# Longer dense runs in a planned instruction order: twelve matmuls to a piece, fewer pages held back, no preference for dense work, and one column moved to ScalarE

## The chip, the cores and the metric

The kernel runs on one core of a Trainium2 chip. The metric is the time of one execution in microseconds (us), as the device reports it; lower is better. TensorE appears as PE, its weight loads as PEld, VectorE as DVE, ScalarE as ACT, GpSimd as POOL and the engine that issues the DMAs as SP.

## The reference

One layer of a streaming encoder on 1024 prompt rows and 32 sample rows of width 1024, float32 throughout. Cut to what matters:

```python
n = rmsnorm(x, lw['norm_mix'])
p = n @ lw['w_in']                                   # 1024 -> 3840 columns
hg_o, hg_s = hgrn2_mixer(p[..., :HG_COLS], ...)      # 4 heads of 128, gated linear recurrence
rw_o, rw_s, rw_shift = rwkv7_mixer(p[..., HG_COLS:], shift0, ...)   # 8 heads of 64
x = x + jnp.concatenate([hg_o, rw_o], axis=-1) @ lw['w_out']
x = x + cross_attend(rmsnorm(x, lw['norm_cross']), mk, mv, lw['w_cq'], lw['w_co'])
n = rmsnorm(x, lw['norm_ffn'])
x = x + (jax.nn.silu(n @ lw['w_ff1']) * (n @ lw['w_ff3'])) @ lw['w_ff2']
```

The first step of the RWKV mixer blends each projected row with the row before it, and this is where the one column comes from:

```python
prev = jnp.concatenate([shift0.astype(p.dtype), p[:, :-1]], axis=1)
xs = (p + (prev - p) * mu).astype(jnp.float32)
```

Both recurrences are computed in chunks, the RWKV one with an inversion of a 64x64 triangular matrix in every chunk and a chain of states from chunk to chunk.

## The kernel before, in words

The 1056 rows lie along the free axis, in three blocks of 352 (`BLOCKS`), four of 264, or chunks of 256, as a stage needs. A weight matrix times activations is a **dense product**: both operands are split into a high and a low float32r part, and `gemm` (or `fast` in the feed-forward) issues three matmuls per 128 rows of contraction: high by high, high by low, low by high. All other matmuls are small: transposes, 64x64 products of the state chain, float16 products of the inversion, scores and values of the attention.

The code does not fix the order of instructions. Every call is recorded as a node of a graph (`Graph.record`). Tensor calls up to the next `nc.cut()` form one node and stay together, so `if i % CUT == 0: nc.cut()` in `gemm` and `k % CUT` in `fast` set the length of a dense piece: with `CUT = 2`, two steps of contraction, six matmuls. `plan` then lists the nodes of all engines greedily in the order of modelled time, and `order` calls it up to `PASSES` times, each time with the latest start times (`latest`) of the result before as ranks, and keeps the pass with the shortest modelled span. The number that it minimises is a model's and is not used here.

What in `plan` bears on the change:

- Phases 0 (projections and mixers) to 6 are open at once within limits (`LEAD`), so dense work of one stage fills gaps in the chains of another.
- When a tensor node is picked, candidates that are ready go by rank. If more than `WARM = 2.0` us of modelled time have passed since the last dense node (`lack`), dense candidates go first.
- On-chip memory is a set of regions cut in pages. A node other than the oldest unfinished one gets pages only if `RESERVE[phase]` pages stay free (a third of it where the node also takes a PSUM bank): 64 in phase 0, 32 in phase 1.
- A tensor node takes one of 8 PSUM banks, kept until its readers are done.

`rw_proj` is the mixing step. For each of 14 column tiles and each block, `mix` reads the projected block from its PSUM bank: ACT writes the block times (1 - mu), DVE adds mu times the block shifted by one column. The first column of a block needs the last of the block before, which ACT keeps as `edge`; DVE adds it in an instruction of one column. In the last block the first sample row takes the shift row of the input (`sh`), again one column on DVE. `params` prepares per-column constants, `mixers` four scaled matrices `rkj`.

In traces and in the instruction order the names are those of the regions: `bank` is a PSUM bank; `f_0`, `mb` hold float32 tiles; `r_0` activations in float32r; `rw` weights in float32r. A PE instruction that reads `rw` is a dense one. All engine calls are issued from one line of `emit` (L378).

Of the kernel before, what the change touches and what calls it, by code (L numbers as in the profile page):

```python
# [30 lines left out]
BIAS = 1e5  # L31
TQ = T // 4
DIAG = 1
CUT = 2
WARM = 2.0
LATER = 10.0
PASSES = 3
KEEP = 1.5 * BIAS
FF_GROUPS = (3, 3, 2, 2)

# [19 lines left out]

REGIONS = {"f0": (192, "left", "FFFFFFF", ()), "wr": (32, "left", "FFFFFFF", ()), "r0": (192, "left", "RRRRRRR", ()), "rw": (64, "left", "RRRRRRR", ()),
           "mb": (256, "left", "FRRRRRR", (150,)), "r1": (64, "right", "RRRRFFF", (150,))}
RESERVE = [64, 32, 24, 24, 24, 24, 24]
AHEAD = {"rw": 1, "rc": 2, "hg": 2, "at": 3}
LEAD = {0: BIG, 1: 400, 2: 250, 3: 400, 4: 100, 5: 200, 6: 60}
HOME = {"keep": ("f0",), "wr": ("wr",), "wh": ("rw",), "wl": ("rw",), "wr2": ("wr",), "wh2": ("rw",), "wl2": ("rw",),
# [231 lines left out]
class Graph:  # L298
# [90 lines left out]
    def order(self):  # L389

        nodes = self.nodes
        for n in nodes:
            if n.calls[0][0] == "memset" and not n.preds:
                later = [u for b in n.bufs for u in b.users if u.i > n.i and u.calls[0][0] != "memset"]
                if later:
                    n.preds.update({p: None for p in min(later, key=lambda u: u.i).preds if p.calls[0][0] != "memset"})
        base = {n: n.cost for n in self.nodes}
        bufs = list(dict.fromkeys(b for n in self.nodes for b in n.bufs))
        best, rank = None, None
        self.log = []  # L400
        for _ in range(PASSES):
            for n in self.nodes:
                n.cost = base[n]
                if n.unit:
                    n.unit[2] = 0
            for b in bufs:
                b.at = None
            try:
                out = self.plan(rank)
            except AssertionError:  # L410
                self.log.append(None)
                break
            self.log.append(self.span)
            if best is None or self.span < best[0]:
                best = self.span, out, [b.at for b in bufs], [(n.start, n.cost) for n in self.nodes]
            rank = self.latest(out)
        self.span = best[0]
        for b, at in zip(bufs, best[2]):
            b.at = at
        for n, t in zip(self.nodes, best[3]):  # L420
            n.start, n.cost = t
        return best[1]

    def latest(self, out):

# [22 lines left out]
    def plan(self, rank):  # L448
# [30 lines left out]
            n.path = n.path - n.bias if rank is None else -rank[n]  # L479
        engines = ("tensor", "vector", "scalar", "gpsimd", "sync")  # L480
        clock = dict.fromkeys(engines, 0.0)
        warm = 0.0
        port = 0.0
        ready = {e: [] for e in engines}
        when = {}
# [76 lines left out]
        def fits(n, start):  # L562

            first = n.i == oldest
            if not first and sum(rest[:n.phase]) > LEAD[n.phase]:
                return None
            if n.unit and not first and n.unit[1] >= base[n.unit[0]] + AHEAD[n.unit[0]]:
                return None
            new = [b for b in n.bufs if b.at is None and b.fixed is None]
            if not new:  # L570
                return start
            for c in FIFO:
                k = sorted(b.turn for b in new if b.cls == c)
                if k and (k != list(range(turn[c], turn[c] + len(k))) or live[c] + len(k) > FIFO[c]):
                    return None
            ps = sum(b.space == "PS" for b in new)
            if ps:
                free = sorted(t for t in banks if t < BIG)
                if len(free) < ps + (0 if first else 2):
                    return None  # L580
                start = max(start, free[ps - 1])
            sb = [b for b in new if b.space == "SB"]
            if sb:
                keep = 0 if first or sb[0].kind == "R" or sb[0].cls in HOME else RESERVE[n.phase] // 3 if any(b.space == "PS" for b in n.bufs) else RESERVE[n.phase]
                if np.count_nonzero((freed < BIG) & pages(sb[0])) < sum(b.units for b in sb) + keep:
                    return None
                for b in sb:
                    if b.at is None:
                        at = place(b, start)
                        if at is None:  # L590
                            return None
                        start = max(start, at[1])
            return start
# [26 lines left out]
        while len(done) < len(nodes):  # L620
            turn_over()
            best = None
            for e in engines:
# [4 lines left out]
                    continue  # L628

                pick = None  # L630
                lack = e == "tensor" and now - warm > WARM
                for t, n in sorted(ready[e], key=lambda r: (max(r[0], now), lack and not r[1].dense, -r[1].path)):
                    t = max(t, now, port) if n.port else max(t, now)
                    if pick is not None and t >= pick[0]:
                        break
                    s = fits(n, t)
                    if s is None:
                        continue
                    if pick is None or s < pick[0]:
                        pick = s, n  # L640
                    if s <= now:
                        break
# [16 lines left out]
            ready[e] = [r for r in ready[e] if r[1] is not n]  # L659
            n.start = start  # L660
            clock[e] = start + n.cost
            if e == "tensor" and n.dense:
                warm = clock[e]
            if n.port:
                port = clock[e] - (0.15 if e == "gpsimd" else 0.0)
            when[n] = start + n.cost + n.late
# [38 lines left out]
class Net:  # L705
# [91 lines left out]
    def params(self):  # L797
# [25 lines left out]
            return self.dp[:, at:at + k]  # L823

        V.tensor_scalar(derived("omu", 0, 14), self.P("mu", 0, 14), -1.0, 1.0, ALU.mult, ALU.add)
        V.tensor_scalar(derived("nkk", 14, 4), self.P("kk", 0, 4), -1.0, None, ALU.mult)
        V.tensor_scalar(derived("nw0", 42, 4), self.P("w0", 0, 4), -1.0, None, ALU.mult)
        V.tensor_scalar(derived("na0", 46, 4), self.P("a0", 0, 4), -1.0, None, ALU.mult)
# [646 lines left out]
    def mixers(self):  # L1475
# [11 lines left out]
        self.rkj = []  # L1487
        for j in range(4):
            self.rkj.append(self.mc.tile([128, 128], F32, name="rkj"))
            nc.vector.tensor_scalar(self.rkj[j], self.j64, self.P("rk", j), None, ALU.mult)  # L1490
        for j in (0, 2):
            self.rwkv(j)
            self.enter(None)
# [48 lines left out]
    def rw_proj(self, tile, done=None, bias=BIAS):  # L1542
# [5 lines left out]
        def mix(t0, n, ps):  # L1548
            nonlocal edge
            m = self.tmp([128, TB], "mixed")[:, :n]  # L1550
            S.activation(m, ps, AF.Copy, scale=self.P("omu", tile))
            c = min(TP - t0, n)
            if t0:
                V.scalar_tensor_tensor(m[:, 0:1], edge, mu, m[:, 0:1], ALU.mult, ALU.add)
            V.scalar_tensor_tensor(m[:, 1:c], ps[:, 0:c - 1], mu, m[:, 1:c], ALU.mult, ALU.add)
            if c == n:
                edge = self.tmp([128, 1], "edge")
                S.copy(edge, ps[:, n - 1:n])
            else:
                S.copy(self.last[:, tile:tile + 1], ps[:, c - 1:c])  # L1560
                S.copy(self.last[:, 14 + tile:15 + tile], ps[:, n - 1:n])
                V.scalar_tensor_tensor(m[:, c:c + 1], self.P("sh", tile), mu, m[:, c:c + 1], ALU.mult, ALU.add)
                V.scalar_tensor_tensor(m[:, c + 1:n], ps[:, c:n - 1], mu, m[:, c + 1:n], ALU.mult, ALU.add)
            if done:
                done(t0, n, m)
            else:
                nc.sync.dma_start(self.p_dram[:, 16 + tile, t0:t0 + n], m)
# [485 lines left out]
```

## Time and profile before

| what | value |
|---|---|
| median of 3 runs | 1875.8 us (1875.39 to 1876.47) |
| the profiled execution | 1872.31 us, of it the span of the trace 1870.6 us |
| mean granted clock of TensorE | 0.988 |
| busy share of PE, DVE, ACT, POOL | 96%, 69%, 44%, 32% |
| matmul records | 15439, of them 9984 dense |
| DMA | 201.88 MB, mean 108 GB/s |

The span runs from the first to the last instruction of the program; about 1.7 us of the execution lie around it. A float32 matmul that is not float32r leaves two records in the trace, so there are more records than matmuls. A timeline row gives the start, the length, the engine, what is written and read, the array's share (rows*columns), the shape and how many; a wait stands behind it in brackets. Matmul records overlap, so the time that a group takes is read from its start to the next group's start.

### The profile page before, as it was taken

Reading aid. Unit: us, or ns where it says so; the run is one execution under the profiler, and the core shown is the slowest. Engines: PE = TensorE matmul, PEld = TensorE weight load, DVE = VectorE, ACT = ScalarE, POOL = GpSimd, SP = SyncE. Lnnn points to the kernel's source line nnn. Section 1 sums busy time; section 2 is a strip of 40 time slices with the busy share of each in tenths; the row PEclk is TensorE's granted clock in tenths of the full one; section 3 lists DMA queues with packets and bytes.
Section 4 is the critical chain, followed back from the end, with each engine's and each line's share of the span. In section 5 each row is a group of like instructions: output and inputs, shape, how many; then the busy total and the mean of one; then the engine's idle time right before and its main releaser. Section 6 shows DMA issues by size and latency. Waiting matters only on the chain. (4 is left out here: it accounts for less than half of the span.)

```text
span 1870.6 us, 39378 instructions
## 1 busy us (share of the span) xinstructions
PE 1798.7 (96%) x15439; PEld 1689.5 (90%) x15439; DVE 1287.8 (69%) x2547; ACT 827.0 (44%) x1938; POOL 594.7 (32%) x764
## 2 busy tenths in 40 slices
PE   6899999999999999999999999999999999999898
PEld 5898888888788888999999999899999999999897
DVE  5347746887766678623654547798877777978997
ACT  5535527465454567633322346333333333653432
POOL 6234234354323433245000024523223223233321
PEclk9999999999999999999999999999999999999999
DMA  6364123222312136844111143133222224644622
GB/s 190 103 193 113 37 79 100 81 69 64 101 49 66 61 101 193 248 139 137 47 46 46 48 149 103 46 113 123 87 94 90 87 102 169 202 146 141 194 69 94
DMA packets 206314, 201.88 MB, mean 108 GB/s; under 512 B 18712, under 2 KB 191376, under 8 KB 206128
## 3 DMA queue, kind: packets, MB, share of 16 engines
q1 hardware_dynamic: 206128, 199.37, 34.3%
q8 instruction: 121, 1.98, 0.5%
q14 instruction: 65, 0.53, 0.1%
HBM read 139.66 MB, written 59.67 MB: 107 GB/s over the span
## 5 line engine op out<-in xcount | busy, mean ns | idle before, releaser
L378 PE MATMUL bank<-r,rw 128*128 128x264 f32 (+1 forms) x5952 | 927.6, 308 | 8.9 <-DVE mb L378 4.1
L378 PEld LDWEIGHTS bank<-r,rw 128*128 128x128 f32 x5952 | 844.8, 189 | 26.6 <-issue 4.6
L378 PE MATMUL bank<-mb,rw 128*128 128x264 f32 (+2 forms) x3648 | 516.9, 296 | 17.3 <-DVE f L378 6.1
L378 PEld LDWEIGHTS bank<-mb,rw 128*128 128x128 f32 x3648 | 486.9, 190 | 25.3 <-ACT rw L378 5.7
L378 DVE TENSOR_TENSOR f<-bank,f 128x264 f32<-128x264 f32 (+6 forms) x541 | 239.6, 459 | 206.3 <-PE bank L378 167.5
L378 DVE TENSOR_TENSOR f<-f 128x264 f32<-128x264 f32 (+8 forms) x348 | 221.6, 656 | 19.1 <-POOL f L378 7.6
L378 POOL TENSOR_TENSOR f<-f 128x64 f32<-128x64 f32 (+8 forms) x237 | 128.0, 553 | 323.4 <-ACT f L378 265.2
L378 ACT CAST rw<-wr 128x512 fp32r<-128x512 f32 (+3 forms) x162 | 113.0, 705 | 242.4 <-PE bank L378 209.3
L378 PE MATMUL bank<-f 128*128 128x128 f32 (+12 forms) x1244 | 185.6, 291 | 2.5 <-DVE f L378 1.0
L378 ACT ACTIVATE f<-f 128x256 f32<-128x256 f32 (+6 forms) x331 | 142.0, 452 | 101.2 <-DVE f L378 47.9
L378 DVE TENSOR_TENSOR mb<-bank,f 128x1024 f16<-128x1024 f32 (+6 forms) x203 | 144.5, 735 | 43.8 <-PE bank L378 33.5
L378 PEld LDWEIGHTS bank<-f 128*128 128x128 f32 (+7 forms) x1244 | 141.7, 160 | 28.1 <-issue 5.5
L378 PE MATMUL bank<-f,mb 128*128 128x64 f16 (+5 forms) x2264 | 121.4, 216 | 25.5 <-POOL f L378 13.9
L378 ACT CAST rw<-r 128x512 fp32r<-128x512 f32 (+2 forms) x128 | 73.3, 574 | 121.9 <-PE bank L378 84.5
L378 ACT COPY mb<-bank 128x512 f32<-128x512 f32 (+5 forms) x175 | 76.7, 455 | 112.7 <-PE bank L378 93.6
L378 DVE TENSOR_TENSOR rw<-r,rw 128x512 fp32r<-128x512 f32 (+2 forms) x128 | 93.4, 733 | 38.0 <-ACT rw L378 37.6
L378 DVE TENSOR_TENSOR rw<-wr,rw 128x512 fp32r<-128x512 f32 (+3 forms) x132 | 102.3, 779 | 14.5 <-ACT rw L378 13.1
L378 ACT COPY f<-bank 128x264 f32<-128x264 f32 (+4 forms) x233 | 72.8, 336 | 88.7 <-PE bank L378 77.0
L378 POOL TENSOR_TENSOR r<-r 128x512 f32<-128x512 f32 (+2 forms) x45 | 66.9, 1493 | 131.9 <-DVE rw L378 67.6
L378 POOL TENSOR_TENSOR rw<-wr,rw 128x1024 fp32r<-128x1024 f32 x30 | 73.2, 2450 | 101.2 <-ACT rw L378 73.1
L378 PE MATMUL bank<-mb 64*64 64x64 f32 (+4 forms) x1556 | 84.5, 236 | 5.0 <-DVE mb L378 4.0
L378 PEld LDWEIGHTS bank<-f,mb 64*64 64x64 f32 (+3 forms) x1176 | 54.5, 139 | 34.5 <-POOL f L378 14.1
(117 smaller groups left out, 1661.6 us busy)
## 6 DMA issues: line engine op xcount, KB each, us to landing
wr<-in_w_in_dram SPq DMA_DIRECT2D x30, 512.0 KB
p_scratch<-mb SPq DMA_DIRECT2D x83, 176.0 KB
wr<-in_w_ff_dram SPq DMA_DIRECT2D x27, 512.0 KB
r<-in_w_ff_dram SPq DMA_DIRECT2D x25, 512.0 KB
f<-h_scratch SPq DMA_DIRECT2D x46, 264.0 KB
h_scratch<-f SPq DMA_DIRECT2D x17, 528.0 KB
h_scratch<-f SPq DMA_DIRECT2D x19, 396.0 KB
f<-x_scratch SPq DMA_DIRECT2D x14, 528.0 KB
```

What stands on the lines that cost most here:

```text
L378: getattr(eng, method)(*args, **kw)
```

## The change

- `CUT` goes from 2 to 4: a dense piece is four steps of contraction, twelve matmuls.
- `RESERVE` falls from 64 and 32 to 16 and 16 pages in phases 0 and 1.
- `WARM`, `warm` and `lack` are gone: ready tensor nodes go by rank alone, ties by number.
- `order` makes two passes and takes the second; it does not compare.
- In the mixing step the first column of a block is formed by ACT in one instruction from the bank, with `edge` (now already multiplied by mu) as bias, and the remaining 351 columns in another. The sample's first column is formed the same way, with a new constant `msh` = mu times the shift row. The four `rkj` are scaled on ACT.

```diff
-CUT = 2
-WARM = 2.0
+CUT = 4
 LATER = 10.0
-PASSES = 3
...
-RESERVE = [64, 32, 24, 24, 24, 24, 24]
+RESERVE = [16, 16, 24, 24, 24, 24, 24]
...
+        return run(self.latest(run(None)))
...
-                lack = e == "tensor" and now - warm > WARM
-                for t, n in sorted(ready[e], key=lambda r: (max(r[0], now), lack and not r[1].dense, -r[1].path)):
+                line = [(max(r[0], now), -r[1].path, r[1].i, r) for r in ready[e]]
+                line.sort()
+                for *_, (t, n) in line:
...
+        V.tensor_tensor(derived("msh", 50, 14), self.P("mu", 0, 14), self.P("sh", 0, 14), ALU.mult)
...
-            nc.vector.tensor_scalar(self.rkj[j], self.j64, self.P("rk", j), None, ALU.mult)
+            nc.scalar.activation(self.rkj[j], self.j64, AF.Copy, scale=self.P("rk", j))
...
-            S.activation(m, ps, AF.Copy, scale=self.P("omu", tile))
+            keep = self.P("omu", tile)
             c = min(TP - t0, n)
             if t0:
-                V.scalar_tensor_tensor(m[:, 0:1], edge, mu, m[:, 0:1], ALU.mult, ALU.add)
+                S.activation(m[:, 0:1], ps[:, 0:1], AF.Identity, scale=keep, bias=edge)
+                S.activation(m[:, 1:n], ps[:, 1:n], AF.Copy, scale=keep)
+            else:
+                S.activation(m, ps, AF.Copy, scale=keep)
             V.scalar_tensor_tensor(m[:, 1:c], ps[:, 0:c - 1], mu, m[:, 1:c], ALU.mult, ALU.add)
             if c == n:
                 edge = self.tmp([128, 1], "edge")
-                S.copy(edge, ps[:, n - 1:n])
+                S.activation(edge, ps[:, n - 1:n], AF.Copy, scale=mu)
...
-                V.scalar_tensor_tensor(m[:, c:c + 1], self.P("sh", tile), mu, m[:, c:c + 1], ALU.mult, ALU.add)
+                S.activation(m[:, c:c + 1], ps[:, c:c + 1], AF.Identity, scale=keep, bias=self.P("msh", tile))
```

The order of nearly the whole program moves with it. Three places show how.

PE in the mixers, where the state chain of the first four RWKV heads runs (64x64 x4 are its products) while projections (128x352) fill in; before:

```order
L378 MATMUL bank_58<-mb_87 64x64 x4
L378 MATMUL bank_63<-r_0_79,rw_83 128x352 x6
L378 MATMUL bank_60<-f_0_71,mb_87 64x64 x4
L378 MATMUL bank_59<-r_0_79,rw_83 128x352 x6
L378 MATMUL bank_64<-mb_87 64x64 x4
L378 MATMUL bank_65<-r_0_79,rw_83 128x352 x6
L378 MATMUL bank_61<-mb_87 64x64 x4
```

The same chain after; the second region `r_0_91` holds the other half of the activations, so its run is printed in pieces:

```order
L376 MATMUL bank_65<-mb_87 64x64 x4
L376 MATMUL bank_59<-r_0_79,rw_83 128x352 x12
L376 MATMUL bank_62<-f_0_71,mb_87 64x64 x4
L376 MATMUL bank_61<-r_0_79,rw_83 128x352
L376 MATMUL bank_61<-r_0_91,rw_83 128x352
L376 MATMUL bank_61<-r_0_79,rw_83 128x352 x2
L376 MATMUL bank_61<-r_0_91,rw_83 128x352
L376 MATMUL bank_61<-r_0_79,rw_83 128x352 x2
L376 MATMUL bank_61<-r_0_91,rw_83 128x352
L376 MATMUL bank_61<-r_0_79,rw_83 128x352 x2
L376 MATMUL bank_61<-r_0_91,rw_83 128x352
L376 MATMUL bank_61<-r_0_79,rw_83 128x352
```

Between two products of the chain stand twelve dense matmuls where six stood.

PE later in the mixers, where the work of a chunk around the chain (x16, x32, 128x512) is at hand; before, and then after, the end of one bunch:

```order
L378 MATMUL bank_60<-f_0_71,mb_87 64x64 x4
L378 MATMUL bank_59<-r_0_79,rw_83 128x352 x6
L378 MATMUL bank_64<-mb_87 64x64 x32
L378 MATMUL bank_62<-mb_87,f_0_71 128x512
L378 MATMUL bank_65<-r_0_79,rw_83 128x352 x6
L378 MATMUL bank_61<-mb_87,f_0_71 128x512
L378 MATMUL bank_58<-mb_87 64x64 x4
```

```order
L376 MATMUL bank_65<-mb_87 64x64 x4
L376 MATMUL bank_64<-mb_87 64x64 x16
L376 MATMUL bank_64<-f_0_71,mb_87 64x64 x16
L376 MATMUL bank_58<-f_0_71,mb_87 64x64 x16
L376 MATMUL bank_63<-mb_87 64x64 x16
L376 MATMUL bank_61<-mb_87,f_0_71 128x512
L376 MATMUL bank_64<-mb_87,f_0_71 128x256 x2
L376 MATMUL bank_62<-r_0_79,rw_83 128x352
```

The dense pieces inside such work are gone; the bunch whose end is shown has 99 small matmuls in a row. Before, one run of small matmuls had 60 or more, of 234; after, thirteen have, the longest 212.

ACT in the first mixing steps, before and after:

```order
L378 ACTIVATE mb_87<-bank_63,f_0_71 128x352
L378 COPY f_0_71<-bank_63 128x1
L378 ACTIVATE mb_87<-bank_65,f_0_71 128x352
L378 ACTIVATE mb_87<-mb_87 64x352
L378 COPY f_0_71<-bank_65 128x1
```

```order
L376 ACTIVATE mb_87<-bank_61,f_0_71 128x351
L376 CAST r_0_79<-bank_64 128x4x32
L376 ACTIVATE mb_87<-bank_61,f_0_71 128x1
L376 ACTIVATE f_0_71<-bank_61,f_0_71 128x1
L376 ACTIVATE mb_87<-mb_87 64x352
```

One instruction more per block reads the bank on ACT; DVE's list loses its one-column instructions (`SCALAR_TENSOR_TENSOR mb_87<-f_0_71,mb_87 128x1`).

More of the change, by code (lines that the diff above doesn't have):

```diff
@@ L396, in order, with run @@
                     n.preds.update({p: None for p in min(later, key=lambda u: u.i).preds if p.calls[0][0] != "memset"})
[L397 to L402, printed above, removed]
+        base = {n: n.cost for n in nodes}
+        bufs = list(dict.fromkeys(b for n in nodes for b in n.bufs))
+        def run(rank):
+            for n in nodes:
                 n.cost = base[n]
@@ L407, in order @@
                 b.at = None
[L408 to L422, printed above, removed]
+            return self.plan(rank)
+        return run(self.latest(run(None)))
     def latest(self, out):
@@ L481, in plan @@
         clock = dict.fromkeys(engines, 0.0)
-        warm = 0.0
         port = 0.0
@@ L571, in fits @@
                 return start
[L572 to L575, printed above, removed]
+            for c in {b.cls for b in new}:
+                if c in FIFO:
+                    k = sorted(b.turn for b in new if b.cls == c)
+                    if k != list(range(turn[c], turn[c] + len(k))) or live[c] + len(k) > FIFO[c]:
+                        return None
             ps = sum(b.space == "PS" for b in new)
@@ L661, in plan @@
             clock[e] = start + n.cost
-            if e == "tensor" and n.dense:
-                warm = clock[e]
             if n.port:
```

## The prediction

> **What bounds the kernel now.** The page comes first: its span and its first section.
>
> ```profile
> span 1870.6 us, 39378 instructions
> PE 1798.7 (96%) x15439; PEld 1689.5 (90%) x15439; DVE 1287.8 (69%) x2547; ACT 827.0 (44%) x1938; POOL 594.7 (32%) x764
> ```
>
> TensorE (PE) is busy for 1798.7 of 1870.6 us; no other engine is above 69%. Only two things can move the time: the 71.9 us in which PE stands idle, and the time that its own stream takes for the same matmuls. The view of busy time by stretches shows where each lies.
>
> ```profile
> 100.00:717.00 617.00, 597.83 (x6497) 519.64 (x6495) 427.58 (x913) 318.20 (x818) 234.29 (x357) 0.99 0.29 83
> 682.80:717.60 34.80, 31.60 (x390) 24.70 (x388) 29.71 (x113) 27.31 (x108) 14.79 (x44) 0.95 0.41 118
> 850.00:1150.00 300.00, 298.41 (x1966) 284.09 (x1964) 155.14 (x372) 106.71 (x264) 52.09 (x53) 1.00 0.27 84
> 1150.00:1250.00 100.00, 92.01 (x702) 90.22 (x702) 84.82 (x129) 43.34 (x96) 45.33 (x36) 0.95 0.22 70
> 1250.00:1600.00 350.00, 349.88 (x2868) 349.91 (x2869) 276.78 (x436) 115.70 (x210) 100.21 (x68) 1.00 0.32 109
> 1600.00:1800.00 200.00, 191.72 (x1541) 189.57 (x1541) 172.10 (x336) 94.38 (x208) 62.60 (x60) 0.99 0.54 168
> ```
>
> The columns are the stretch, its length, busy time of PE, weight loads, VectorE (DVE), ScalarE (ACT) and GpSimd, the granted clock, DMA share and GB/s. The two mixers run from 100 to 717 us: PE is idle there for 19.2 us, and the stream is a weave of dense runs (float32r projections) with small matmuls. From 850 us on, attention and the feed-forward leave PE 1.6 idle in 300 us and 0.1 in 350. The holes at 1150 to 1250 (8.0 us, DVE busy 85%) and 1600 to 1800 (8.3 us, DVE 86%) belong to operands that DVE prepares; dense runs of another length give DVE no less to do. So I expect the change to act between 100 and 800 us.
>
> **Run length.** The new order holds the same 9984 dense and 3631 small matmuls. The dense ones stand in 191 unbroken runs where they stood in 289, so there are 98 fewer interruptions. By the kind of small matmul ahead of the dense run, 26 fewer follow float16, 33 fewer follow those that fill only part of the array (64 rows or 64 columns), 39 fewer follow full float32 ones. The timeline of PE prices each; a group's time is from its start to the next group's start.
>
> ```profile
> 133.96 1.79 PE L378 MATMUL bank<-f,mb 64*64 64x64 f32 x48
> 135.68 3.17 PE L378 MATMUL bank<-r,rw 128*128 128x352 f32 x18
> 138.69 0.41 PE L378 MATMUL bank<-f,mb 128*128 128x64 f16 x8
> 138.93 1.21 PE L378 MATMUL bank<-r,rw 128*128 128x352 f32 x6
> 139.98 0.41 PE L378 MATMUL bank<-f,mb 128*128 128x64 f16 x8
> ...
> 147.62 2.17 PE L378 MATMUL bank<-r,rw 128*128 128x352 f32 x12
> 149.64 0.41 PE L378 MATMUL bank<-f,mb 128*128 128x64 f16 x8
> ...
> 170.56 2.18 PE L378 MATMUL bank<-r,rw 128*128 128x352 f32 x12
> 172.67 0.45 PE L378 MATMUL bank<-f,mb 64*64 64x64 f32 x8
> 173.05 1.23 PE L378 MATMUL bank<-r,rw 128*128 128x352 f32 x6
> ...
> 179.43 1.22 PE L378 MATMUL bank<-r,rw 128*128 128x352 f32 x6
> 180.58 2.06 PE L378 MATMUL bank<-f 64*128 64x128 f32 x32
> ```
>
> - Behind float16: six take 1.05 us (138.93 to 139.98), twelve take 2.02 (147.62 to 149.64). Twelve in one run save 2 x 1.05 - 2.02 = 0.08; 26 x 0.08 = 2.1 us.
> - Behind 64x64: six take 1.15 (179.43 to 180.58), twelve 2.11 (170.56 to 172.67), a saving of 0.19. On the small side, eight alone take 0.38 (172.67 to 173.05) and 48 together 1.72 (133.96 to 135.68), 0.29 for eight: 0.09 more. I use 0.28 for all part-array kinds: 33 x 0.28 = 9.2 us.
> - Behind full float32 the next rows show nothing to save: eight transposes take 0.76 and the six dense ones 1.07, where eighteen took 3.01, or 1.00 for six. That is at most 0.07, 2.7 us for 39; the dense run starts while the transposes still drain, so I take 0.
>
> ```profile
> 680.99 0.82 PE L378 MATMUL bank<-f 128*128 128x128 f32 x8
> 681.75 1.23 PE L378 MATMUL bank<-r,rw 128*128 128x352 f32 x6
> 682.82 0.41 PE L378 MATMUL bank<-f,mb 128*128 128x64 f16 x8
> ```
>
> Part comes back. Small groups that a dense run held apart now stand side by side: changes from one small kind straight to another go from 286 to 333, 47 more. Such a change costs between 0 and the 0.28 above, so 0 to 13 us. I take 0.10, near the float16 price, since many of them involve full or float16 groups: 4.7 us. Net 2.1 + 9.2 - 4.7 = 6.6 us less, all of it in PE's own stream, which nothing hides.
>
> **Waits in the mixers.** These are PE's waits from 100 to 800 us, by who ended them (total, times, longest).
>
> ```profile
> PE bank L378 <- ACT mb L378: 7.4, 6, 3.6
> PE bank L378 <- DVE mb L378: 6.9, 7, 2.4
> PE bank L378 <- DVE f L378: 3.7, 3, 1.7
> PE bank L378 <- ACT f L378: 1.3, 3, 0.7
> ```
>
> With four small ones they make 20.6 us. Six waits above 1 us hold 12.3; they end chains of several instructions, and I leave them. The other 8.3 us are short misses. I counted, in both orders, the round trips in which PE waits for one DVE or ACT instruction that itself waited for PE: with less than 1 us of PE work in between there were 75, now there are 34, because twelve dense matmuls stand where six stood. I halve the short misses: 4 us less (bounds 0 and 8.3).
>
> Against it: without the preference for dense products, small work bunches. Stretches without a dense matmul of more than 3.4 us, counted by those durations, go from 2 to 33; in the mixers they hold 106 us more. PE has no cover in them. The row of 682.8 to 717.6 is such a stretch, the final burst of the mixers: 3.2 us idle in 34.8, 0.09 per us. That gives 106 x 0.09 = 9.5 us as the far end. The near end is 0: the stretch from 187.3 (next fence) has 6.49 busy of 6.50. I take a third, 3 us, as most bunches are wide parallel groups like the latter.
>
> **Mixing step.** 42 one-column instructions leave DVE and 42 join ACT.
>
> ```profile
> L378 DVE SCALAR_TENSOR_TENSOR mb<-f,mb 128x1 f32<-128x1 f32 x42 | 14.7, 378 | 0.0
> L378 ACT COPY f<-bank 128x1 f32<-128x1 f32 x38 | 4.7, 167 | 3.3 <-DVE mb L378 3.2
> ```
>
> DVE loses 14.7 us; ACT gains 42 x 0.17 = 7 us while it is busy 318 of 617. Each PSUM bank of a projection is read by one more ACT instruction; a bank is held 0.17 us longer, while DVE's later pass over the other columns still ends last. What is late next would be ACT's own evacuations. Of the 6.9 us of waits on DVE mb I credit 1 (bounds 0 and 5). The multiplication of the four bonus matrices and the new product of mu and the shift row run before 100 us once and count 0; the many other instructions around them cover them. One table load fewer on ACT counts 0 as well.
>
> **Fewer pages held back** has no duration of its own: it lets later work start earlier, and what that does to PE is in the counts above. Sum: -6.6 - 4 + 3 - 1 = -8.6, say 9 us. The profiled execution took 1872.3 us, which becomes 1863; the median of the runs shown is 3.5 above it at 1875.8, so I forecast 1867.
>
> **The clock.** Here a rule speaks against the change. Four rows by stretches:
>
> ```profile
> 87.80:91.20 3.40, 2.78 (x26) 2.54 (x24) 1.52 (x5) 3.23 (x10) 3.23 (x2) 1.00 0.04 13
> 187.30:193.80 6.50, 6.49 (x131) 5.82 (x131) 5.84 (x13) 2.06 (x4) 3.85 (x6) 1.00 0.06 17
> 238.10:241.50 3.40, 3.40 (x23) 2.78 (x22) 3.31 (x5) 0.26 (x1) 3.24 (x4) 0.50 0.19 38
> 698.90:702.30 3.40, 3.34 (x42) 2.88 (x42) 3.33 (x12) 3.01 (x13) 0.40 (x2) 0.50 0.37 120
> ```
>
> Two of PE's timeline:
>
> ```profile
> 236.31 0.52 PE L378 MATMUL bank<-mb,f 64*64 64x64 f32 x8 [2.02 <-DVE mb L378]
> 238.43 2.13 PE L378 MATMUL bank<-r,rw 128*128 128x352 f32 x6
> ```
>
> Half clock comes in 3.4 us pieces. The piece at 238.1 follows a wait of 2.02 us; six dense matmuls then take 2.13 instead of 1.22, so a piece costs about 1.5 us. A stretch of small matmuls alone kept the full clock where PE was busy (187.3, 6.5 us; and the 3.4 us from 87.8), and the 34.8 us burst drew one piece, at 698.9. So by the rows, bunching costs clock only through waits, about 106/34.8 = 3 pieces, 4.5 us at the far end; I take 0, since the short waits fall. The Trainium skill, "TensorE: Matmul & The Clock Gate", Part 4, says that transposes do not count as PE work for the full rate. By that rule bunches with many transposes would go cold; the row from 87.8, mostly transposes at clock 1.00, does not bear it out for so short a bunch.
>
> **Rivals.**
> - *No measurable change* (0.2): the 47 small changes cost 0.2 each and bunched waits reach their far end: -11.3 + 9.4 - 4 + 9.5 - 1 = +2.6; with half of that cost -3, so about 1876. For it: both unknowns have wide bounds. Against: the dense saving is read from rows and cannot be hidden.
> - *Slower by the clock* (0.1): half of the 31 added stretches fall to half clock, 16 x 1.5 = 24 - 9 = +15, 1891. It decides from six pieces more than now. For it: pieces follow idle of 1 to 2 us, and bunches have no cover. Against: 187.3.
> - *Slower by waits* (0.1): bunches turn into chains. The 34.8 us burst loses 0.09 per us; at twice that 106 us cost 19, -6.6 - 1 + 19 = +11, 1887.
> - *More than forecast* (0.1): the mixers' waits go altogether, 6.6 + 20.6 = 27, 1849. For it: fewer tight trips. Against: the six long waits are chains.
>
> **How the numbers follow.** The forecast has 0.5, its own range -4 to -16 (1860 to 1872). Faster by over 0.2% (3.8 us, about what this measurement can tell) has 0.5 + 0.1, same 0.2, slower 0.2. The range, 1852 to 1883, holds the forecast and the case of no change with their bounds, and leaves out the fast rival's far half and most of the two slow ones, under 0.2 in all.
>
> **What would show it.** In the new profile, the six-long dense groups between 100 and 717 us should be gone and the mixers should end about 8 us sooner; waits of PE from 100 to 800 should be near 19 us; the one-column rows of DVE should be missing; the rest should have moved as a block. If instead the clock of that stretch is below 0.98, or waits exceed 30 us, the forecast is wrong by its bunches.

## The result and the profile after

The changed kernel takes 1857.4 us (median of 4 executions, 1856.23 to 1861.43) where the kernel before takes 1875.6 (4 executions on the same chip). The ratio is 0.9908, 95% interval 0.9891 to 0.9925: 18.2 us faster by the medians, 0.9% by the ratio. The forecast was 1867, 9 us faster. The profiled executions, 1872.3 and 1857.1 us, differ by 15.3 us; the rest of the 18.2 is that the one of before lies 3.3 below its median.

The page of the changed kernel, its span and first section:

```profile
span 1855.3 us, 39311 instructions
PE 1787.0 (96%) x15439; PEld 1688.6 (91%) x15439; DVE 1273.5 (69%) x2502; ACT 839.4 (45%) x1983; POOL 596.8 (32%) x764
```

PE works 11.7 us less for the same 15439 records; 45 small instructions left DVE (2547 to 2502) and 45 joined ACT. Stretches of the changed kernel, with the columns of the prediction's table:

```profile
100.00:717.00 617.00, 596.55 (x6520) 526.26 (x6519) 434.98 (x901) 337.00 (x879) 243.25 (x384) 0.97 0.29 85
850.00:1150.00 300.00, 299.15 (x1997) 285.56 (x1996) 158.99 (x396) 114.04 (x290) 49.35 (x50) 1.00 0.27 83
1150.00:1250.00 100.00, 92.14 (x726) 90.47 (x725) 83.59 (x126) 35.95 (x69) 48.96 (x37) 0.97 0.26 86
1250.00:1600.00 350.00, 350.00 (x2870) 350.00 (x2870) 273.95 (x432) 119.26 (x217) 95.83 (x68) 1.00 0.32 106
1600.00:1800.00 200.00, 193.40 (x1570) 191.84 (x1569) 175.29 (x357) 94.45 (x209) 64.87 (x62) 1.00 0.51 159
```

The first row is the stage on which the sum was made, and it is no better: 20.5 us idle where there were 19.2, clock 0.97 instead of 0.99. To see where the time went I cut both traces at the same places of the program, in two cases at the same dense matmul (the last projection, and the next dense product after it), and set each stage's time against its matmuls' **slots**: each matmul counted with the time from start to start that its form takes in an undisturbed row of the kernel before (0.161 us for 128x352 float32r, 0.122 for 128x264, 0.029 for float16, 0.036 for 64x64). What is left is the **loss** of the stage: waits, half clock, changes of kind. In us:

| loss in | load | mixers | burst | out_proj | cross | end | tail | sum |
|---|---|---|---|---|---|---|---|---|
| before | 32.5 | 84.2 | 12.7 | 13.2 | 9.6 | 21.9 | 7.8 | 181.9 |
| after | 32.2 | 76.1 | 20.0 | 5.2 | 6.5 | 18.2 | 8.4 | 166.6 |
| difference | -0.3 | -8.1 | +7.3 | -8.0 | -3.1 | -3.7 | +0.6 | -15.3 |

Each trace is one execution. "Load" is about the first 100 us, "tail" what follows the last matmul, "burst" the dense-free stretch behind the last projection, "out_proj" the stage from there to the output projection's norm, "cross" attention up to its own norm, "end" the rest with the feed-forward. Three rows show the first half of the trade: the mixers up to the burst (of before, then after), then the burst of after.

```profile
100.00:682.80 582.80, 566.82 (x6120) 495.46 (x6118) 398.47 (x801) 291.49 (x712) 219.49 (x313) 0.99 0.28 81
```

```profile
100.00:679.00 579.00, 563.72 (x6182) 500.30 (x6181) 406.45 (x807) 310.07 (x785) 226.88 (x340) 0.99 0.29 84
679.00:720.40 41.40, 36.24 (x365) 28.59 (x364) 31.50 (x103) 29.52 (x102) 17.01 (x45) 0.75 0.36 105
687.00:707.50 20.50, 18.35 (x184) 14.68 (x183) 15.53 (x51) 12.85 (x39) 10.10 (x22) 0.51 0.25 71
```

PE reaches the last projection 3.8 us sooner although 62 more matmul records lie ahead of it. The burst then takes 41.4 us where before's (682.8 to 717.6) took 34.8 with 25 records more: it waits 5.2 us instead of 3.2, and for 20.5 us PE is granted half its clock, where one piece of 3.4 us was seen before. Between the burst and the norm of the output projection, before and after:

```profile
717.60:900.10 182.50, 177.56 (x1234) 171.15 (x1232) 88.64 (x164) 88.63 (x203) 70.92 (x92) 1.00 0.56 177
```

```profile
720.40:891.00 170.60, 169.19 (x1195) 165.32 (x1194) 75.11 (x136) 76.35 (x167) 59.14 (x65) 1.00 0.58 181
```

This stage is 11.9 us shorter: 39 fewer small records lie in it (3.9 us of slots, done earlier now), its waits go from 4.9 to 1.4 us, and its loss from 13.2 to 5.2.

### The profile page after: what moved, and what is told of

Same layout as the page of the kernel before. It is cut to its first block, busy times and chain, and to the rows that moved or that the text cites. A ratio compares the mean times of both kernels' runs of the same rounds, so it can differ in the third digit from the quotient of the medians.

```text
span 1855.3 us, 39311 instructions
## 1 busy us (share of the span) xinstructions
PE 1787.0 (96%) x15439; PEld 1688.6 (91%) x15439; DVE 1273.5 (69%) x2502; ACT 839.4 (45%) x1983; POOL 596.8 (32%) x764
## 5 line engine op out<-in xcount | busy, mean ns | idle before, releaser
L376 PE MATMUL bank<-r,rw 128*128 128x264 f32 (+1 forms) x5952 | 899.9, 306 | 19.2 <-DVE f L376 9.6
L376 PE MATMUL bank<-mb,rw 128*128 128x264 f32 (+3 forms) x3648 | 500.8, 293 | 2.8 <-DVE f L376 1.2
L376 DVE TENSOR_TENSOR f<-f 128x256 f32<-128x256 f32 (+9 forms) x314 | 200.3, 657 | 23.0 <-ACT f L376 16.2
L376 ACT ACTIVATE f<-f 128x256 f32<-128x256 f32 (+5 forms) x326 | 136.6, 443 | 122.7 <-DVE f L376 77.4
L376 PE MATMUL bank<-f 128*128 128x128 f32 (+14 forms) x1354 | 189.6, 286 | 1.7 <-DVE r L376 1.0
L376 PEld LDWEIGHTS bank<-f 128*128 128x128 f32 (+6 forms) x1294 | 143.0, 160 | 29.2 <-issue 5.5
L376 ACT COPY mb<-bank 128x512 f32<-128x512 f32 (+6 forms) x156 | 70.6, 467 | 75.0 <-PE bank L376 57.9
L376 DVE TENSOR_TENSOR rw<-r,rw 128x512 fp32r<-128x512 f32 (+2 forms) x108 | 76.4, 708 | 34.1 <-ACT rw L376 33.4
L376 ACT COPY f<-bank 128x264 f32<-128x264 f32 (+9 forms) x216 | 72.9, 358 | 54.4 <-PE bank L376 42.1
L376 PE MATMUL bank<-mb,f 128*64 128x64 f32 (+9 forms) x496 | 76.6, 330 | 0.8 <-DVE mb L376 0.8
```

The costliest lines, as they stand in the source:

```text
L376: getattr(eng, method)(*args, **kw)
```

## The experiments

**Theory 1** is the prediction's: interruptions of dense work set the time. **Theory 2**: what matters is how long the projections last as cover for the mixers' chains; what is left of the chains then runs bare, and loses waits and clock. A third view, formed later: the planner's order scatters, and no one part owns the gain.

**What one interruption costs.** Three pairs put extra small matmuls into the first feed-forward of the changed kernel: in one of a pair they stand together behind the fourth step of contraction, in the other one half of them stands behind the second step. Same work, 308 interruptions more. With the added matmuls part of the first feed-forward's products is left out of the computation, so a run is read against its partner alone.

```diff
+                    if nk == 4 and k in (3,):        # the other of the pair: k in (1, 3), range(2)
+                        for g in range(4):
+                            for hf in (slice(0, 64), slice(64, 128)):
+                                nc.tensor.matmul(x[hf, 384:448], lhsT=self.ident0[hf, hf], rhs=self.ident0[hf, hf], ...)
```

> The changed kernel, with eight 64x64 matmuls on unused PSUM columns added behind the twelfth dense matmul of each of the 308 nodes of the first feed-forward products. It is the base for the next run, which puts the same work in two places. Eight such matmuls took 0.38 us between dense runs, and the dense run behind them 0.11 us more, so 308 x 0.5 = 154 us on top of 1857: about 2011 us.

> The same added work as e1_km_joined, four 64x64 matmuls behind the sixth and four behind the twelfth dense matmul: 308 interruptions more, nothing else. Theory 1 (an interruption has a price of its own, 0.28 us for part-array matmuls, as the prediction took it): 308 x 0.28 = 86 us above e1_km_joined. Rival (the price read from the mixers was short waits of the chains and not the interruption itself): within 10 us of e1_km_joined.

2093.0 joined, 2199.0 apart: 105.95 / 308 = 0.344 us for one behind 64x64 matmuls. The prediction had 0.28. The joined kernel itself took 82 us more than expected: eight of these matmuls leave 16 records, and the 0.38 us of the expectation belong to a row of eight records, which are four matmuls.

> The changed kernel with eight float16 matmuls (128 rows, 128 columns, 64 wide) behind the twelfth dense matmul of the same 308 nodes. Eight took 0.24 us between dense runs and the dense run behind them 0.08 more: 308 x 0.32 = 99 us, about 1956 us.

> The same float16 work in two places, four and four. Theory 1: 308 x 0.08 = 25 us above e3_h_joined. Rival: within 5 us of it.

1960.3 and 1986.2: 0.084 us behind float16, where 0.08 was read from the rows.

> The kernel changed, plus 308 pairs' worth of full float32 matmuls (128x128) in the first feed-forward: two behind every fourth dense matmul of a group, so that they stand side by side. They leave the first feed-forward's products out of the computation in part, so the time is read against its partner alone. Its partner places one behind the second and one behind the fourth: the same work, 308 more interruptions. Theory A (the prediction: an interruption by full float32 matmuls costs 0 to 0.07 us): partner minus this 0 to 22 us. Theory B (it costs what a part-array one does, 0.34): about 106 us. Theory C (as float16, 0.084): about 26 us.

> As the run before, with one added full float32 matmul behind the second and one behind the fourth dense matmul instead of both behind the fourth: 308 more interruptions with the same work. Theory A (0 to 0.07 us each): 0 to 22 us above the joined kernel. Theory B (0.34 each): 106 above. Theory C (0.084 each): 26 above.

1980.35 and 1982.57: 2.2 / 308 = 0.007 us behind full float32 matmuls, nothing that single runs can tell from 0.

Apart from the added ones, the matmuls stand in the same sequence in both kernels of a pair, and their traces give nearly the same prices without the rest of the run. By medians, twelve dense matmuls and what is added to them take 2.272 us joined and 2.612 apart with 64x64 (0.340), 1.794 and 1.888 with float16 (0.094), 1.910 and 1.910 with full float32 (0). So the prediction's prices hold for float16 and full float32, and 64x64 costs about a fifth more than it took; the other part-array kinds were not tried.

The six kernels also repeat the changed one: up to the first feed-forward, at about 1137 us, their matmuls stand in its order. From the same matmul to the same matmul, their mixers up to the burst took 577.9 to 579.4 us (578.9 in the changed kernel) and their burst 41.2 to 41.7 (41.4), with 17.1 to 20.5 us at half clock. So what the burst costs belongs to the order and is no accident of one execution. The burst of the first of them:

```profile
677.80:719.20 41.40, 36.14 (x364) 28.51 (x363) 31.39 (x103) 29.51 (x102) 17.05 (x44) 0.75 0.35 105
```

**One part alone, on the kernel before.**

```diff
-CUT = 2
+CUT = 4
```

> The kernel before with dense pieces of twelve alone. Its order has 216 dense runs (289 before, 191 in the changed kernel), but the projections are used up sooner: by durations, the small matmuls left over after the last of them stand for 77 us without a dense one (26 before, 23 in the changed kernel). Theory 1 (the number of interruptions sets the time): 73 fewer x 0.12 to 0.19 = 9 to 14 us less, about 1864 us. Theory 2 (what counts is how long dense work lasts as cover; a stretch without it loses clock and waits, as the final burst does in both kernels: 34.9 us for 22.2 us of matmuls before, 41.5 for 21.5 after): 77 us lose half as much again, about 40 us, where the burst before lost 13, so 27 - 11 = 16 us more, about 1890 us.

```diff
-                lack = e == "tensor" and now - warm > WARM
+                lack = False
```

> The kernel before without the preference for dense products alone. 272 dense runs, and no stretch without dense work above 12 us: the final burst is gone. Theory 1: 17 fewer runs, 2 to 3 us less, about 1873 us. Theory 2: the 12.7 us that the burst loses beyond its matmuls are saved, about 1862 us.

```diff
-RESERVE = [64, 32, 24, 24, 24, 24, 24]
+RESERVE = [16, 16, 24, 24, 24, 24, 24]
```

> The kernel before with 16 pages held back in phases 0 and 1 instead of 64 and 32, alone. 298 dense runs, final burst of 17.5 us instead of 25.6. Theory 1: 9 more runs, 1 us more, about 1877 us. Theory 2: a third of the burst's loss less, -4 us, about 1872 us.

**One part undone (or taken further) in the kernel after.** The lines are those of the change, put back: `WARM` and `lack`, `CUT = 2`, the old `RESERVE`, the old mixing step; and `CUT = 8`, of which no line is in the change.

> The changed kernel with the preference for dense products put back, alone. 209 dense runs instead of 191, the final burst 41 us instead of 23 by durations. Theory 1: 18 runs more, 2 to 3 us, about 1860 us. Theory 2: the burst loses 20 us for 21.5 us of matmuls in the changed kernel, so about 18 us more, about 1875 us.

> The changed kernel with dense pieces of six again, alone. 245 dense runs instead of 191; 24.5 us of small matmuls are left over after the last projection, about as in the changed kernel (23). Theory 1 with the prices measured by e1 to e4 (0.34 us behind part-array matmuls, 0.08 behind float16): 26 more part-array interruptions x 0.34 + 15 x 0.08 = 10 us, less 47 fewer changes between small kinds (up to 5 us): 5 to 10 us more, 1862 to 1867 us. Theory 2 adds nothing here, since the final burst is the same.

> The changed kernel with 64 and 32 pages held back again, alone. 195 dense runs, as good as the changed kernel's 191, but 76 us of small matmuls left over after the last projection. Theory 1: about 1 us, 1858 us. Theory 2: as in e5_cut4, whose burst of that length lost 97 us where the changed kernel's lost 20: about 70 us more, 1925 us.

> The changed kernel with the mixing step's first column on DVE again, alone. 193 dense runs, burst of 23 us: both theories expect nothing from the order. The prediction credited this part with 1 us, so 1858 us, within 0.2%.

> The changed kernel with dense pieces of twenty-four. 130 dense runs instead of 191, but 69 us of small matmuls left over after the last projection. Theory 1: 61 fewer runs, 22 of them behind part-array and 15 behind float16 matmuls, 22 x 0.34 + 15 x 0.08 = 9 us less 3 for small changes: about 1851 us. Theory 2: the burst loses some 85 us instead of 20: about 1915 us.

Measured, as ratios to the kernel before on the same chip, with the loss of four stages:

| kernel | us | ratio, 95% interval | mixers | burst | out_proj | end |
|---|---|---|---|---|---|---|
| before | 1872 to 1876 | 1 | 84.2 | 12.7 | 13.2 | 21.9 |
| after | 1857.4 | 0.9908 (0.9891 to 0.9925) | 76.1 | 20.0 | 5.2 | 18.2 |
| before, `CUT` 4 | 1928.0 | 1.0299 (1.0284 to 1.0315) | 61.1 | 97.1 | 20.4 | 18.4 |
| before, no `WARM` | 1876.0 | 1.0023 (1.0011 to 1.0035) | 84.3 | none | 25.9 | 28.9 |
| before, fewer pages | 1881.3 | 1.0046 (1.0030 to 1.0062) | 80.3 | 28.9 | 15.8 | 19.0 |
| after, `WARM` back | 1880.1 | 1.0051 (1.0031 to 1.0070) | 74.0 | 35.4 | 13.5 | 19.3 |
| after, `CUT` 2 | 1923.3 | 1.0262 (1.0240 to 1.0284) | 83.8 | 31.8 | 35.4 | 25.3 |
| after, pages back | 1933.2 | 1.0323 (1.0308 to 1.0339) | 53.7 | 101.1 | 22.2 | 17.3 |
| after, old mixing step | 1871.5 | 0.9992 (0.9982 to 1.0002) | 82.2 | 16.8 | 16.6 | 18.9 |
| after, `CUT` 8 | 1907.2 | 1.0187 (1.0158 to 1.0215) | 50.4 | 69.2 | 35.4 | 12.9 |

No part does it alone: none of the three tried alone is a gain, and each of the four undone takes the whole gain away. (The planner's two passes without comparison were not undone by themselves.) Theory 1 fails for the total: it had 1864 us for `CUT` 4 alone (216 dense runs) and 1851 for `CUT` 8 (130). The loss in their mixers does fall, by 23 and 34 us, but most of that is work that left the stage: it holds 3191 and 2807 small records instead of 4301, and at before's 19.6 ns of loss for each, that is 22 and 29 us. What bears Theory 1 out inside the mixers are the kernels that keep nearly all small work there (3900 to 4400 records). With waits and lost clock taken off, their loss is 62 to 64 us with 209 and 218 dense runs in the stage, 56 with 179, and 50 to 55 with 136 to 138. The burst of `CUT` 4 alone, by stretch and by PE's waits (total, times, longest):

```profile
602.40:771.50 169.10, 122.52 (x1402) 98.46 (x1400) 129.05 (x290) 90.23 (x258) 56.22 (x125) 0.75 0.13 38
```

```profile
PE bank L378 <- DVE mb L378: 19.2, 18, 4.3
PE bank L378 <- DVE f L378: 18.5, 16, 3.4
PE bank L378 <- ACT mb L378: 4.4, 6, 1.2
```

The projections are spent 80 us sooner (602.4 instead of 682.8), and 72 us of small matmuls are left to run bare. They take 169 us: 46.6 waiting on chains through DVE and ACT, and half of the time at half clock. That is Theory 2 in kind, though it had 1890 us: the 72 us lost 97 and not 40. Its values for pages back (172.6 us bare), `CUT` 8 (134.5) and `WARM` back came within 9 us. But a burst is not all: without `WARM` there is none, and the loss reappears in out_proj and the end, for no gain, where Theory 2 had 1862. Fewer pages alone leave less bare work than before, 17 us of slots, and lose 28.9 there instead of 12.7. And for two runs Theory 2 had nothing at all. `CUT` 2 and the old mixing step, both put back in the changed kernel, leave about as much bare work as after (23.4 and 21.5 us of slots, after 21.5), and are still 66 and 16 us above it by ratio, with out_proj as the stage that lost most. Their rows of that stage, `CUT` 2 first:

```profile
738.30:941.00 202.70, 187.72 (x1260) 179.11 (x1259) 92.70 (x186) 94.42 (x226) 73.81 (x103) 0.94 0.51 161
```

```profile
713.60:894.00 180.40, 173.01 (x1222) 167.24 (x1221) 87.75 (x170) 90.16 (x215) 71.23 (x93) 0.99 0.56 176
```

They wait 15.0 and 7.4 us where the changed kernel waits 1.4, and hold 228 and 192 small records where it holds 124: more of the mixers' last chains runs on beside the output projection. Over all kernels with a burst the loss of out_proj goes with that number: 5.2 to 6.3 us with 104 to 124 (the changed kernel and two runs below), 13.2 and 13.5 with 162 and 166 (before, `WARM` back), 16.6 with 192, and 15.8 to 35.4 with 228 to 827. The last runs ask what makes the bare clock fall, and how much of this is the order alone.

**Dense cover put back into the burst.**

```diff
+                if node.eng == "tensor" and first < at < until:
+                    for b in node.bufs:
+                        if b.space == "PS" and b.elems <= 256:
+                            for _ in range(FILL):        # FILL = 2
+                                real.tensor.matmul(self.banks[b.at][:, 256:512], lhsT=fill[:, 0:128], rhs=fill, start=True, stop=True)
```

> The changed kernel, with two more float32r matmuls (128x256, into the unused half of the small matmul's own bank) behind each of 28 small groups between the last projection and the next dense product; they compute nothing that is used. They add 56 x 0.12 = 6.7 us of slots and 28 interruptions. Theory A (the lack of dense work is itself what halves the clock there): the 20.5 us at half clock go, the granted clock of 679 to 720 rises from about 0.75 to 0.95 or more, that gives back 10 us; the matmuls and their interruptions (28 x 0.344 = 9.6) partly fill the 5.2 us of waits: 1853 to 1862. Theory B (the clock falls because PE waits for chains, and dense cover does not change that): the clock stays near 0.75, the added work is paid: 1866 to 1875.

> The kernel before with twelve matmuls in a row alone (1928), with the same two float32r matmuls behind each of 82 small groups of its 169 us without a dense product; they compute nothing that is used. They add 164 x 0.12 = 20 us of slots and 82 x 0.344 = 28 us of interruptions. Theory A (lack of dense work halves the clock): the 86 us at half clock there go, the granted clock rises to 0.95 or more, 43 us come back, and the 46.6 us of waits hide most of the added work: 1885 to 1915. Theory B (waiting halves the clock): the clock stays below 0.85 and the time is 1928 to 1960.

1865.6 us (ratio 0.9958, 0.9943 to 0.9973) and 1952.3 (1.0432, 1.0408 to 1.0455). The bursts, of the filled changed kernel and the filled `CUT` 4:

```profile
679.50:724.00 44.50, 40.92 (x424) 33.30 (x423) 31.84 (x104) 30.02 (x102) 17.51 (x47) 0.92 0.34 99
```

```profile
603.40:791.50 188.10, 147.29 (x1569) 119.66 (x1568) 127.90 (x292) 92.07 (x258) 53.89 (x125) 0.78 0.12 35
```

The two answers differ. In the short burst the clock rises from 0.75 to 0.92 (half-clock time 20.5 to 6.8 us) and waits fall from 5.2 to 3.6; the burst is still 3.1 us longer, since the cover costs more than it brings. In the long one 40.8 us of waits remain and the clock stays at 0.78. So the clock of a bare stretch goes with its waits as far as this: the two bursts with under 10% idle had 0.95 (before) and 0.92 (this one); those with 12 to 28% had 0.55 to 0.83. Among the latter the idle share doesn't order the clock: 0.55 came with 16% (fewer pages alone), 0.83 with 25% (`CUT` 8). Dense matmuls beside long waits did not hold it up here. Which of the two lifted it in the short burst, the cover or the shorter waits, these runs can't separate.

**The column's engine, in the same order.** 42 one-column additions issued on VectorE, with nothing else of the order changed:

```diff
+                    if method == "activation" and args[2] == AF.Identity and node.calls[0][1][0].shape[1] == 1:
+                        real.vector.scalar_tensor_tensor(args[0], args[1], kw["scale"], kw["bias"], ALU.mult, ALU.add)
+                        continue
```

> The changed kernel with its order of instructions kept as it is, except that the 42 one-column additions of the mixing step run on VectorE instead of ScalarE. Undoing that step in the planner's input as well gave 1871.5, 14 us more than the changed kernel. Theory A (the engine that computes the column matters): most of the 14 us comes back, 1865 to 1872. Theory B (the order that the planner made of it matters, the column is worth the 1 us that the prediction gave it): 1855 to 1860.

1861.5 us, ratio 0.9948 (0.9931 to 0.9965): by medians 4 us, by ratios 7.5 us slower than the changed kernel, where undoing the step in the planner's input as well cost 14 to 16. Neither theory is met. Out_proj's loss stays at 5.3 here and was 16.6 there, so that part is the order's. Whether the 4 to 7.5 us are the column's is not shown: from the same matmul to the same matmul, mixers and burst together, where the column is formed, take 620.0 us in this trace and 620.3 in that of the changed kernel; 2.4 of the 3.4 us between the two spans lie in the end.

**A nudge.**

```diff
-FREE_PS, FREE_SB = 0.2, 0.2
+FREE_PS, FREE_SB = 0.2, 0.21
```

> The changed kernel with one cost of the planner nudged, the time after which a freed SBUF page may be taken, 0.20 to 0.21 us. No work is added or taken away: dense runs 188 (191), small changes 338 (334), 193 us in stretches without a dense product (194). Only the last such stretch differs: 32.4 us of slots instead of 23.1. Theory A (the number of interruptions sets the time): 1855 to 1860. Theory B (the last dense-free stretch sets it; so far each us of its slots cost about 1 us of waits and lost clock): 9 more, 1863 to 1870. Theory C (an order is good to some 10 us either way by chance, in load, mixers and the output stage alike): anything from 1848 to 1878, with losses that move in stages outside that stretch by 5 us or more.

1878.8 us, ratio 1.0037 (1.0021 to 1.0053): a hundredth of a microsecond in a cost of the planner costs 21 us, more than the whole change brought. Interruptions (188 for 191) don't tell it. Its burst:

```profile
676.00:735.90 59.90, 48.05 (x513) 38.83 (x511) 49.27 (x150) 39.00 (x129) 19.80 (x58) 0.77 0.30 86
```

The projections end 3 us sooner than in the changed kernel and 28.6 us of slots are left bare instead of 21.5; the burst's loss rises from 20.0 to 31.2, as Theory 2 has it. Another 6.1 us come in the end (24.3 for 18.2), where the matmuls stand in the same sequence of forms, and 3.7 in the mixers, as the third view has it. It is slower than any of the three expectations allowed. Out_proj keeps its gain (6.3). Of the four parts undone, the mixing step (14 us) and `WARM` (23) therefore moved the time hardly more than a nudge that means nothing; `CUT` (66) and the pages (76) moved it clearly more. Only one nudge was tried.

## Why the prediction was right or wrong

The sign was right and the range of 1852 to 1883 held the time; the forecast's own range, 1860 to 1872, did not, and the size was half of what came. In the stages for which the sum was made, 0.8 us came instead of 8.6. That the kernel is faster is owed to stages for which the sum had no term, so the sign was in good part luck.

- **Run length, -6.6:** borne out. In the mixers the loss falls by 8.1 us; 0.7 of it is waits (16.0 to 15.3), and the time at half clock is 13.7 us in both, so 7.4 is the stream. The prices are 0.084, 0.344 and 0.007 us by the pairs, for 0.08, 0.28 and 0. The price of changes between small kinds was not tried by itself.
- **Waits, -4, and bunches, +3:** each about half of what came, and that their sum held is luck. From 100 to 800 us PE's waits went from 20.6 to 19.7 us, where I had said near 19. The short misses that I halved, those up to 1 us, are 18 in both kernels and went from 8.3 to 7.0 us. But the waits moved. By the traces, the mixers of before have five stretches of over 3.4 us without a dense matmul ahead of the burst, which hold 6.1 of the stage's 15.1 us of listed waits; after there are 24, and they hold 13.4 of 14.5 and all of the stage's half clock. So the waits in the bunches rose by 7.3 us, and those outside fell from 8.9 to 1.1. The largest waits from 100 to 700 us, where they rose from 16.8 to 18.2, of before, then of the changed kernel:

```profile
PE bank L378 <- DVE mb L378: 6.1, 6, 2.4
PE bank L378 <- ACT mb L378: 5.5, 4, 3.6
PE bank L378 <- DVE f L378: 3.7, 3, 1.7
```

```profile
PE bank L376 <- DVE f L376: 6.7, 6, 4.1
PE bank L376 <- DVE mb L376: 5.2, 8, 2.8
PE bank L376 <- DMA mb<-in_x_prompt_dram: 3.4, 1, 3.4
PE bank L376 <- ACT f L376: 1.8, 2, 1.1
PE bank L376 <- ACT mb L376: 0.9, 1, 0.9
```

Waits on `mb` by DVE and ACT went from 11.6 to 6.1 together, but those on DVE's `f` rose by 3.0 and a load of 3.4 came late. I took fewer tight round trips for fewer waits; most of what was saved came back in the bunches.
- **Bunches and the clock, 0:** the row that I took as proof that bunches are free, 187.3 to 193.8, is none: six dense matmuls stand in it from 189.91. Most bunches ahead of the last burst are indeed free. One of 8.3 us, of 109 records, has no wait and the full clock:

```profile
285.47:293.78 8.31, 8.31 (x109) 6.47 (x107) 2.73 (x7) 4.71 (x11) 3.53 (x5) 1.00 0.28 87
```

The two dearest are not, one with the late load, one with a wait of 4.1 us on DVE:

```profile
115.20:129.20 14.00, 10.58 (x118) 9.37 (x117) 7.83 (x16) 6.85 (x20) 11.04 (x7) 0.76 0.74 207
582.30:591.70 9.40, 5.28 (x41) 3.63 (x41) 7.15 (x13) 1.77 (x3) 5.08 (x10) 0.64 0.35 97
```

The last burst alone lost 7.3 us more, on about the same slots (21.5 and 22.2), mostly by its clock. I had judged the clock from that same burst of before, where it drew one piece, and the rival "slower by the clock" spread its pieces over all bunches; the place was the burst.
- **Mixing step, -1:** not settled. The same order with the column on VectorE is 4 to 7.5 us slower, around the far bound of 5, but its trace doesn't show that where the column is formed. The price was misread: I took the 0.17 us of a `COPY`, and the new instructions take 0.36 each on ACT, which is busy 12.4 us more where I had 7:

```profile
L376 ACT ACTIVATE mb<-bank,f 128x1 f32<-128x1 f32 x42 | 13.4, 362 | 1.0 <-DVE mb L376 1.0
```

- **Nothing behind the burst ("the rest should have moved as a block", "I expect the change to act between 100 and 800 us"):** this is the step that failed. Mixers and burst together gave 0.8 us. Of the other 14.5, 14.2 lie behind 720 us, about 5 of them before 800, and there I had no term, on the ground that dense runs of another length give DVE no less to do. Out_proj's 8.0 came with less of the mixers' small work left beside it: 124 small records in the stage instead of 162; 3.5 of the 8.0 are waits. That can be counted in the order ahead of time; I had costed no row of that stage. Cross gave 3.1: its waits fell from 4.1 to 2.3 us, and one piece of 3.4 us at half clock, from 1152.9 in before, has no counterpart after. Why is open: its loss is 5.6 to 8.9 in the kernels of the table with `CUT` of 4 or 8 and 7.9 to 10.5 in those with 2, and these overlap. The end's 3.7 isn't shown to belong to the change: the last 5274 matmuls stand in the same sequence of forms in both kernels and after the nudge, and the loss there was 21.9 before, 20.6 with the changed kernel's order but for the column, and 24.3 after the nudge.

Of the rivals, "more than forecast" (1849) is about as near in size as the forecast, but its mechanism, no waits in the mixers, did not come.

Of the marks that I had named, the six-long dense groups and the one-column rows of DVE are gone, and the waits are near 19 us. The projections ended 3.8 us sooner instead of 8, but the mixers' burst 2.8 later (720.4 instead of 717.6); the clock from 100 to 717 fell to 0.97, below the 0.98 that was to prove the bunches mis-sized; and the rest did not move as a block.

So the gain that I forecast did come in the stream, was eaten by the burst, and was given back twice over behind it. That this order leaves less of the chains beside the output projection is measured. That a neighbouring order keeps the whole gain is not: the nudge kept this part and lost more elsewhere.

## What to carry to other kernels

Where a planner sets the order, the price of a local effect (here 0.08 to 0.34 us for an interruption) can be right and still not tell the time: look at what lasts to the end as cover for the chains, count what is left bare behind the last dense product, and what of it spills into the next stage. Try a change of a planner's rules with a neutral nudge beside it: one of 0.01 us moved the time by 21 us here, so a gain of 18 us shows a good order and not a good rule. Undoing each part showed more than doing each alone, as no part was a gain by itself, but it too has to be held against the nudge.

## What the runs showed of the hardware

- Half clock can last. It came in multiples of 3.41 us: one piece of 20.5 us in the burst of the changed kernel, 41.0 us in those of fewer pages alone and of `CUT` 2 put back. PE was busy for 18.35 of those 20.5 us, and the longest wait in the whole burst was 1.4 us. Two rows of its timeline:

```profile
699.38 0.69 PE L376 MATMUL bank<-mb 64*64 64x64 f32 x8
700.00 1.22 PE L376 MATMUL bank<-f 128*128 128x128 f32 x4
```

Eight records of 64x64 matmuls take 0.62 us from start to start; the eight at 172.67 in the prediction's rows took 0.38. The burst of fewer pages alone, where a piece of 41.0 us fills nearly all of it:

```profile
674.70:720.50 45.80, 38.38 (x381) 31.36 (x380) 35.44 (x100) 25.91 (x89) 15.69 (x43) 0.55 0.31 89
```

The Trainium skill, "TensorE: Matmul & The Clock Gate", under "HAM oscillation — how this bites in real kernels", gives the rule that idle gaps above about 3.4 us cost the clock; no gap in the burst was that long. Its next section, "A second HAM failure mode: psum-queue depth-cycling", says that frequent micro-idles between groups of matmuls make the clock oscillate. The burst is nearer to that one, with 5.2 us idle in 41.4 in pieces of at most 1.4 and a clock of 0.75, but its clock stayed at half in one piece instead of oscillating.
- The price of an interruption depends on what interrupts: 0.344 us behind 64x64 matmuls, 0.084 behind float16, 0.007 behind full 128x128 float32 (0.340, 0.094 and 0 by the medians of the traces).
